# Two of the three passes of the experts' gate and up products made as one 512-column matmul

## The chip, the cores and the metric

The kernel runs on one core of one Trainium2 chip. The metric is the device time of an execution in microseconds; several runs of the same program are taken and their median is compared. Every product of the kernel is float32 in quality: operands are split into a high and a low part, and float32r passes of TensorE (PE in the profile) are summed in PSUM.

## The reference, cut to what matters

The program is one layer of an encoder: mixers (a long convolution, neighbourhood attention, pooling), an output projection, and then a mixture of 16 experts where each expert chooses 256 of the 2048 tokens. Only the experts matter here:

```
aff = softmax(h @ w_router)
gate, idx = top_k(aff.T, 256)          # per expert
xs = h[idx]                            # 16 x 256 x 1024
a = xs @ w_gate                        # 1024 -> 2048, per expert
b = xs @ w_up                          # 1024 -> 2048, per expert
y = (silu(a) * b) @ w_down * gate      # 2048 -> 1024, per expert
out = scatter-add of y at idx
```

## The kernel before, in words

The kernel works through stages: input projections, filter and convolution, attention, output projection and router, the search for each expert's tokens, and the experts (method `experts`, from L1055). This text deals with the last of them.

**Weights.** Each expert's weights (24 MB) come from HBM in 24 pieces of 1 MB. Helper `weights` (L1073) issues the transfer on SP's queue into `mo_raw`, and `split` (L208) makes two parts: ScalarE (ACT) copies to float32r `mo_wh` (L210), VectorE (DVE) subtracts to get `mo_wl` (L211). `mo_raw`, `mo_wh` and `mo_wl` have three buffers each, so the parts of a piece can be made once PE is done with the piece three before it.

**Gate and up.** For each eighth `f` of the 2048 hidden columns there are two pieces, first of w_gate, then of w_up. This text calls the work of one piece a tile. A tile has two halves `m` of 128 hidden columns, 8 chunks `d` of the 1024 inputs, and three passes each, by `mm3` (L213 to L217): 48 matmuls with the weights stationary and 256 tokens moving. `mm3` is

```
mm(out, lhsT=lh, rhs=rh, ...)   # L215: high weights, high tokens
mm(out, lhsT=lh, rhs=rl, ...)   # L216: high weights, low tokens
mm(out, lhsT=ll, rhs=rh, ...)   # L217: low weights, high tokens
```

The sums of a tile, 128 x 2 x 256, fill one PSUM bank. The tag `mm` has 6 banks, `tp` has 2 for transposes (L1332). After both tiles of an `f`, ACT applies Silu from PSUM to `mo_s` (L1149), DVE multiplies by the other bank (L1150), and `split` writes the parts `mo_hh` and `mo_hl` for the down product.

**Down.** Eight pieces of w_down, each with 24 matmuls of 512 columns by the same `mm3`, sum into four banks. ACT scales them into `mo_y` (L1172), and POOL adds the rows to the accumulator in DRAM (L1173).

**Lookahead.** At f = 3 the program emits the next expert's tokens: DVE makes 16 one-hot arrays (L1085), PE turns them into indices by 32 tiny matmuls (L1089), DVE finishes the indices (L1095), POOL issues two gathers of 128 rows, `mo_xg` (L1101). When they land, PE transposes them, four 128 x 128 blocks to a bank, two banks for each gather (L1117), and `split` writes `mo_xh` and `mo_xl`. DVE also copies the gate column from each gather (`mo_gt`, L1121).

What sets the order on each engine is a planner that simulates the program as it is emitted. Each engine then executes its own list in that order. Thus an instruction that waits also holds all behind it on its engine.

Of the kernel before, what the change touches and what calls it, by code (L numbers as in the profile page):

```python
# [33 lines left out]
def _parts(m):  # L34
    """Two parts of a float32 array of at most 12 significant bits each."""
    m = np.ascontiguousarray(m).astype(np.float32)
    h = ((m.view(np.uint32) + np.uint32(0x800)) & np.uint32(0xFFFFF000)).view(np.float32)
    return h, m - h


def _consts():
    """Arrays that depend on the shapes alone."""
# [31 lines left out]
    # rows (s, cs, n2), columns (cs', s, k2)  # L74
    z = np.zeros((4, 2, 16, 2, 4, 16))
    # rows (cs', s, k2), columns (s, cs, n2)
# [14 lines left out]
    # slot 0: frequency 0 and 2048; slots 1..7: 256 k2; slots 8..15: 128 + 256 (k2 - 8)  # L91
# [48 lines left out]
    # the candidates of a search by base-4 digits: four phases of 4, 4, 4 and 3 digits, each phase  # L140
    # in units of 2**-9 of the phase before
    # and half a unit less than the last of them
# [11 lines left out]
def _layouts(a):  # L154
    """Small inputs side by side, each in its own type, and the position biases in reverse."""
    f = np.zeros((128, 451), np.float32)
    f[0:33, 0:64] = a["hy_f_w1"][0]
    for h in range(2):
        r = slice(h * 64, h * 64 + 64)
        f[r, 64 + h * 64:128 + h * 64] = a["hy_f_w2"][0]  # L160
        f[r, 192:448] = a["hy_f_wout"][0][:, h * 256:h * 256 + 256]
        for q, n in enumerate(("hy_f_b1", "hy_f_b2", "hy_f_freq")):
            f[r, 448 + q] = a[n][0]
    g = np.zeros((128, 258), np.float32)
    for k in range(4):
        r = (k % 2) * 64
        g[r:r + 64, (k // 2) * 128 + r:(k // 2) * 128 + r + 64] = a["pool_w"][0][k]
    g[:, 256:258] = a["pool_scale"][0].reshape(2, 128).T
    h = np.zeros((128, 26), np.float32)
    h[:, 0:18] = a["hy_short_w"][0].reshape(3, 6, 128).transpose(2, 1, 0).reshape(128, 18)  # L170
    h[:, 18:24] = a["hy_short_b"][0].reshape(6, 128).T
    h[:, 24:26] = a["hy_skip"][0].reshape(2, 128).T
    rpb = a["na_rpb"][0][:, ::-1, ::-1].reshape(2, 4, 15, 31).transpose(0, 2, 1, 3)
    return {"par_f": f, "par_p": g, "par_h": h, "rpb_r": np.ascontiguousarray(rpb).reshape(120, 31)}


def _bc(ap, n, rows=128):
    """A DRAM vector of n elements, the same on every partition."""
    return bass.AP(tensor=ap.tensor, offset=ap.offset, ap=[[0, rows], [1, n]])


class Trunk:
# [16 lines left out]
    def rms(self, pool, ss, n, w):  # L199
        """rstd from sums of squares over n elements."""  # L200
        a = self.sb(pool, [128, w], f"rms_a{w}", bufs=2)
        self.nc.gpsimd.tensor_scalar(a, ss, 1.0 / n, EPS, op0=OP.mult, op1=OP.add)
        r = self.sb(pool, [128, w], f"rms_r{w}", bufs=2)
        self.nc.gpsimd.tensor_tensor(r, a, self.mhalf[:, 0:w], op=OP.pow)
        self.mark = self.nc.cur_bb.bb.instructions[-1]
        return r

    def split(self, hi, lo, src):  # L208
        """hi + lo = src exactly, each with at most 12 significant bits."""
# [9 lines left out]
    # ------------------------------------------------------------------ input projections  # L219
    def prep(self, pool, early, chunk, out):  # L220
        """x -> RMS norm, transposed and split, for 512 tokens."""
# [25 lines left out]
    def proj(self, pool, early):  # L247
        """x -> RMS norm -> w_in, 1024 tokens at a time; every product as three float32r passes."""
# [33 lines left out]
    def copy_values(self, half):  # L282
        """One copy of the values for each block of key columns."""
# [4 lines left out]
    def slab(self, pool, s, m, chunk, wh, wl, hh, hl):  # L288
        """Half a slab of columns of w_in for 512 tokens."""
# [18 lines left out]
        if s in (3, 4):  # L308
            # negated and scaled queries, in the order (column block, row, column)
# [24 lines left out]
    # ------------------------------------------------------------------ long filter and its spectrum  # L334
    def filt(self, pool):
# [13 lines left out]
        def sine(out, src, b):  # L349
            # the argument in turns, less its nearest whole number  # L350
# [61 lines left out]
    def to_groups(self, ev, dst, a, n0, pa):  # L412
        """Rows (k1, part) of two residues go to DRAM as [group][(k1 of 4, part, n2)][channel]."""
# [4 lines left out]
    # ------------------------------------------------------------------ hyena  # L418
    def hyena(self, pool):
# [49 lines left out]
        for g4 in range(8):  # L469
# [3 lines left out]
            # the real parts and the imaginary parts of the filter, each in both halves  # L473
# [8 lines left out]
            else:  # L482
                # frequencies 0 and 2048 share a slot and are real
# [57 lines left out]
    # ------------------------------------------------------------------ pooling  # L541
# [49 lines left out]
    # ------------------------------------------------------------------ neighbourhood attention  # L591
# [4 lines left out]
    def bias_tables(self, pool):  # L596
        """Negated position biases for each kind of column block and each first row of a window, rows
        and columns of keys in descending order: [first row][(query column, half of the heads)]
        [7 rows of BIG, the window, 7 rows of BIG][head][key column]."""
# [7 lines left out]
        # first query, number, offset of the window, offset among the biases: both step with the query  # L607
# [25 lines left out]
    def load_bias(self, tb, hg, rb, cb):  # L633
        """The biases of one block of queries for four heads, [key row][head][key column], over the 15 key
        rows around the block; only the query rows for which they differ from the block before."""
# [3 lines left out]
        # first query row, number, first window row and its step, first row of the source and its step,  # L639
        # first row of the tile, number of rows  # L640
# [8 lines left out]
    def attention(self, kpool, get_pool):  # L649
# [6 lines left out]
        # the low parts of the queries meet the high parts of the keys only  # L656
# [14 lines left out]
        def load(u):  # L671
            """Keys, queries and biases for four heads, eight rows and two blocks of columns."""
# [4 lines left out]
            if g == 0:  # L677
                k = kb([128, 4, 960], "at_k", R, 2)
                have = 0
                if rb:  # L680
                    # rows that the window shares with the one before it
# [43 lines left out]
        for u, (hg, rb, g) in enumerate(units):  # L725
# [16 lines left out]
            for j, cb in enumerate(self.QB[g * 2:g * 2 + 2]):  # L742
# [5 lines left out]
                for h in range(4):  # L748
# [26 lines left out]
                    else:  # L775
                        # two heads at a time, each in its half of the array's columns
# [5 lines left out]
                    if h == 3:  # L782
                        nc.scalar.activation(o[:, :, :, c0:c0 + 16], po.rearrange("p a (r c) -> p a r c", r=8), AF.Copy)
                        if g and j:
# [4 lines left out]
                            # what each query's exponentials sum up to goes into the norm's input  # L789
# [13 lines left out]
    # ------------------------------------------------------------------ output projection, router  # L803
    def load_wo(self, pool):
        """w_out, its rows scaled by the gains of the mixers' norms."""
# [23 lines left out]
    def mix(self, pool, chunk, bufs=1):  # L829
        """The outputs of the mixers for 256 tokens, split, and the rstd of each mixer."""  # L830
# [32 lines left out]
    def out_proj(self, pool, ready):  # L863
# [3 lines left out]
        # the router's weights, their rows scaled by the gains of the norm, both parts side by side  # L867
# [12 lines left out]
        def route(chunk, tiles, xh, xl, rs):  # L880
            """Affinities of one or two tiles of tokens."""
# [13 lines left out]
            else:  # L895
                # the last tile the shorter way
# [60 lines left out]
    # ------------------------------------------------------------------ the 256 tokens of each expert  # L957
    def top_tokens(self, pool):
        """Exact: the 256th largest affinity by a search over its bits, equal ones by token order."""
# [11 lines left out]
        def digits(ph):  # L971
            # a part of the 30 bits as a whole number of at most 8 bits, in the units of its phase
# [13 lines left out]
        for ph, n in enumerate(DIGITS):  # L986
            if ph == 0:
                v = part[0]
            else:
                # above the threshold so far: more than any candidate; below it: less than zero  # L990
# [5 lines left out]
            for k in range(n):  # L996
                # two candidates are counted, of the third the numbers below it less those above it
# [28 lines left out]
        # slots: first those above the threshold, then those on it, each in token order from 1;  # L1026
        # what lies on it beyond the capacity gets a slot above the capacity
# [26 lines left out]
    # ------------------------------------------------------------------ experts  # L1054
    def experts(self, pool):  # L1055
# [50 lines left out]
        def lookahead(e):  # L1106
            """The tokens of expert e, transposed and split."""
            idx, xg = tokens(e)
            gate = sb([128, 2], "mo_gt", F, 2)
            xh = sb([128, 8, 256], "mo_xh", R, 2)  # L1110
            xl = sb([128, 8, 256], "mo_xl", R, 2)
# [10 lines left out]
            return idx, gate, xh, xl  # L1122
# [6 lines left out]
        for e in range(NE):  # L1129
            idx, gate, xh, xl = nxt  # L1130
            hh = sb([128, 16, 256], "mo_hh", R, 1)
            hl = sb([128, 16, 256], "mo_hl", R, 1)
            for f in range(8):
# [6 lines left out]
                for src in (wg, wu):  # L1140
                    w, wlo = weights(src[e, :, :, f * 256:f * 256 + 256])
                    pt = self.bank("mm", (128, 2, 256))
                    for m in range(2):
                        ms = slice(m * 128, m * 128 + 128)
                        for d in range(8):
                            self.mm3(pt[:, m, :], w[:, d, ms], wlo[:, d, ms], xh[:, d, :], xl[:, d, :], d == 0, d == 7)
                    acc.append(pt)
                s = sb([128, 2, 256], "mo_s", F, 2)
                nc.scalar.activation(s, acc[0], AF.Silu)  # L1149
# [4 lines left out]
            po = [[self.bank("mm") for n in range(2)] for h in range(2)]  # L1154
# [44 lines left out]
    # ------------------------------------------------------------------ all of it  # L1199
    def run(self, stages=("all",), dbg=None):  # L1200
        tc, nc = self.tc, self.nc
        from contextlib import ExitStack
        with ExitStack() as st:
# [36 lines left out]
            def steps(gen, n=None):  # L1240
                """Advance a generator by n steps or to its end."""
# [90 lines left out]
            psa = psum("psum_d", mm=6, tp=2)  # L1332
# [32 lines left out]
```

## Time and profile before

| what | us |
|---|---|
| median of 3 runs | 3441.17 |
| lowest and highest run | 3441.08, 3451.25 |
| span of the profiled execution | 3444.6 |

The profiled execution has no separate time beside its span: from its first to its last instruction it took 3444.6 us, 3.4 us more than the median and inside the range of the runs. PE is busy 95% of it, DVE 51%, ACT 40%. Since matmuls overlap in the records and their ends are modelled, what counts for PE is the step from one start to the next.

### The profile page before, as it was taken

What the parts mean: (1) busy time and instruction counts of PE and PEld (TensorE: products, weight loads), DVE (VectorE), ACT (ScalarE), POOL (GpSimd) and SP (SyncE); (2) the same over time, 40 slices, a digit from 0 to 9 for tenths busy, and PEclk for the clock granted to TensorE, in tenths of its full rate; (3) what the DMA queues carried; (4) which work ended last, traced back from release to release, by engine and by line L of the source; (5) the groups of instructions that cost most, each with busy time, mean ns of one, the idle gap of its engine ahead of it and who ended that gap; (6) DMA issues with size and microseconds to landing.
All of it is one profiled execution on the core that took longest, in us unless ns stands there. A gap on an engine that the chain in (4) does not pass through costs nothing.

```text
span 3444.6 us, 52588 instructions
## 1 busy us (share of the span) xinstructions
PE 3267.8 (95%) x21970; PEld 2940.5 (85%) x21970; DVE 1747.9 (51%) x2296; ACT 1379.7 (40%) x1748; POOL 386.2 (11%) x466
## 2 busy tenths in 40 slices
PE   8999999687999599999999999999999999999998
PEld 6888887465688499899999999999989999899997
DVE  5124456254576654454544545545455454454455
ACT  4134422254432344444444444443434444444354
POOL 1212212121211000010010000100001001000011
PEclk9999999797999699999999999999999999999999
DMA  6675697887454356566566665665656656566586
GB/s 218 215 253 191 214 306 251 182 183 167 146 170 140 127 195 201 191 197 200 192 196 197 195 197 192 199 200 181 203 188 197 203 189 205 184 199 199 181 288 238
DMA packets 455158, 685.99 MB, mean 199 GB/s; under 512 B 27447, under 2 KB 366117, under 8 KB 454537
## 3 DMA queue, kind: packets, MB, share of 16 engines
q1 hardware_dynamic: 397592, 537.77, 50.4%
q0 software_dynamic: 28432, 103.26, 10.2%
q10 hardware_dynamic: 28896, 41.61, 3.5%
q8 instruction: 172, 2.82, 0.3%
q14 instruction: 66, 0.53, 0.0%
HBM read 578.05 MB, written 114.83 MB: 201 GB/s over the span
## 4 chain that ended last, share of the span: by engine, by line
PE 69%; issue 16%; DMA 12%; DVE 2%; ACT 0%; SPq 0%; POOL 0%; POOLq 0%; DVEq 0%; ACTq 0%
PE mm L215 20%; PE mm L217 20%; PE mm L216 20%; DMA mo_xg<-Hr,mo_ix 4%; DMA at_t<-Ce 4%; PE o L779 1%; DMA t<-Hd 1%; PE tp L765 1%; PE tp L1117 1%; PE s L752 0%; DMA at_v<-Vc 0%; DMA at_q<-QHd 0%; PE tp L395 0%; PE fl L529 0%; DVE tk_ge L1001 0%
## 5 line engine op out<-in xcount | busy, mean ns | idle before, releaser
L211 DVE TENSOR_TENSOR mo_wl<-mo_raw,mo_wh 128x2048 fp32r<-128x2048 f32 x384 | 879.9, 2292 | 798.4 <-ACT mo_wh L210 798.4
L210 ACT ACTIVATE mo_wh<-mo_raw 128x2048 fp32r<-128x2048 f32 x384 | 735.3, 1915 | 1210.8 <-issue 764.1
L215 PE MATMUL mm<-mo_xh,mo_wh 128*128 128x256 f32 x4096 | 1163.6, 284 | 0.0
L216 PE MATMUL mm<-mo_xl,mo_wh 128*128 128x256 f32 x4096 | 1162.5, 284 | 0.0
L217 PE MATMUL mm<-mo_xh,mo_wl 128*128 128x256 f32 x4096 | 1162.3, 284 | 0.0
L215 PEld LDWEIGHTS mm<-mo_xh,mo_wh 128*128 128x128 f32 x4096 | 788.3, 193 | 0.8 <-ACT mo_xh L210 0.2
L216 PEld LDWEIGHTS mm<-mo_xl,mo_wh 128*128 128x128 f32 x4096 | 788.4, 192 | 0.6
L217 PEld LDWEIGHTS mm<-mo_xh,mo_wl 128*128 128x128 f32 x4096 | 788.4, 192 | 0.0
L215 PE MATMUL mm<-mo_wh,mo_hh 128*128 128x512 f32 x1024 | 398.5, 389 | 0.0
L216 PE MATMUL mm<-mo_wl,mo_hh 128*128 128x512 f32 x1024 | 398.5, 389 | 0.0
L217 PE MATMUL mm<-mo_wh,mo_hl 128*128 128x512 f32 x1024 | 398.3, 389 | 0.0
L1173 POOL DMA_INDIRECT Acc<-mo_y,mo_ix x30 | 76.1, 2538 | 1412.8 <-ACT mo_y L1172 1292.6
L217 PEld LDWEIGHTS mm<-mo_wh,mo_hl 128*128 128x128 f32 x1024 | 192.2, 188 | 40.1
L215 PEld LDWEIGHTS mm<-mo_wh,mo_hh 128*128 128x128 f32 x1024 | 192.3, 188 | 39.6
L216 PEld LDWEIGHTS mm<-mo_wl,mo_hh 128*128 128x128 f32 x1024 | 192.3, 188 | 39.2
L215 PE MATMUL mm<-hT_h,w_h 128*128 128x512 f32 x512 | 205.7, 404 | 2.1 <-ACT hT_h L210 1.7
L216 PE MATMUL mm<-hT_l,w_h 128*128 128x512 f32 x512 | 205.3, 401 | 0.0
L217 PE MATMUL mm<-hT_h,w_l 128*128 128x512 f32 x512 | 204.3, 399 | 0.0
L1150 DVE TENSOR_TENSOR mo_s<-mo_s,mm 128x512 f32<-128x512 f32 x128 | 87.9, 687 | 183.5 <-PE mm L217 183.5
L1101 POOL DMA_INDIRECT mo_xg<-Hr,mo_ix x32 | 62.8, 1963 | 625.9 <-DVE mo_ix L1095 621.0
L215 PEld LDWEIGHTS mm<-hT_h,w_h 128*128 128x128 f32 x512 | 96.4, 189 | 26.0 <-ACT hT_h L210 2.4
L216 PEld LDWEIGHTS mm<-hT_l,w_h 128*128 128x128 f32 x512 | 96.3, 188 | 25.3 <-issue 2.8
(303 smaller groups left out, 3760.2 us busy)
## 6 DMA issues: line engine op xcount, KB each, us to landing
mo_raw<-in_w_gate SPq DMA_DIRECT2D x128, 1024.0 KB
mo_raw<-in_w_up SPq DMA_DIRECT2D x128, 1024.0 KB
mo_raw<-in_w_down SPq DMA_DIRECT2D x128, 1024.0 KB
w_r<-in_w_in SPq DMA_DIRECT2D x40, 512.0 KB
x<-in_x SPq DMA_DIRECT2D x16, 512.0 KB
Ud<-e ACTq DMA_DIRECT2D x32, 256.0 KB
at_q<-QHd SPq DMA_DIRECT2D x32, 256.0 KB
wo_x<-in_x SPq DMA_DIRECT2D x16, 512.0 KB
```

Source lines behind the costliest of these rows:

```text
L210: self.nc.scalar.activation(hi, src, AF.Copy)
L211: self.nc.vector.tensor_tensor(lo, src, hi.bitcast(F), op=OP.subtract)
L215: mm(out, lhsT=lh, rhs=rh, start=start, stop=False)
L216: mm(out, lhsT=lh, rhs=rl, start=False, stop=False)
L217: mm(out, lhsT=ll, rhs=rh, start=False, stop=stop)
L765: nc.tensor.transpose(pt[0:n * nkc, ci, :], s[:, x * nkc:(x + n) * nkc], self.ident)
L779: nc.tensor.matmul(po[hh % 2 * 64:hh % 2 * 64 + 64, h // 2, :], lhsT=v[0:n * nkc, ci, hh * 64:hh * 64 + 64], rhs=pp[0:n * nkc, ci, :], sta ...
L1101: nc.gpsimd.indirect_dma_start(out=g, out_offset=None, in_=self.Hr, in_offset=bass.IndirectOffsetOnAxis(ap=idx[:, h:h + 1].bitcast(U32), a ...
L1117: nc.tensor.transpose(pt[:, d, :], xg[h][:, dd * 128:(dd + 1) * 128], self.ident)
L1150: nc.vector.tensor_tensor(s, s, acc[1], op=OP.mult)
L1173: nc.gpsimd.indirect_dma_start(out=self.Acc, out_offset=off, in_=y, in_offset=None, compute_op=OP.add)
```

## The change: what it does

The high and low parts of the tokens are written side by side into one tile `mo_xx`. For each chunk, the high weights meet both parts in one matmul with 512 moving columns; its two halves go to the two halves of one PSUM bank. The low weights meet the high tokens as before, 256 columns, and add to the second half. So a tile has 32 matmuls instead of 48, with the same number of columns, and its sums take two banks. They are added when they are evicted: ACT copies the second half of both banks to `mo_s`, and DVE adds the first halves to it, once for gate and once for up. Silu and the multiplication then read SBUF. `mo_s` gets three buffers; the six banks become three pairs, and the down product takes two pairs. The rest of the diff removes comments.

```
-            xh = sb([128, 8, 256], "mo_xh", R, 2)
-            xl = sb([128, 8, 256], "mo_xl", R, 2)
+            xx = sb([128, 8, 2, 256], "mo_xx", R, 2)
+            xh, xl = xx[:, :, 0], xx[:, :, 1]
...
-                    pt = self.bank("mm", (128, 2, 256))
+                    pt = self.bank("mm", (128, 2, 2, 256))
                     for m in range(2):
                         ms = slice(m * 128, m * 128 + 128)
                         for d in range(8):
-                            self.mm3(pt[:, m, :], w[:, d, ms], wlo[:, d, ms], xh[:, d, :], xl[:, d, :], d == 0, d == 7)
-                    acc.append(pt)
-                s = sb([128, 2, 256], "mo_s", F, 2)
-                nc.scalar.activation(s, acc[0], AF.Silu)
+                            nc.tensor.matmul(pt[:, m].rearrange("p k t -> p (k t)"), lhsT=w[:, d, ms],
+                                             rhs=xx[:, d].rearrange("p k t -> p (k t)"), start=d == 0, stop=False)
+                            nc.tensor.matmul(pt[:, m, 1], lhsT=wlo[:, d, ms], rhs=xx[:, d, 0], start=False, stop=d == 7)
+                    a = sb([128, 2, 256], "mo_s", F, 3)
+                    nc.scalar.activation(a, pt[:, :, 1], AF.Copy)
+                    nc.vector.tensor_tensor(a, a, pt[:, :, 0], op=OP.add)
+                    acc.append(a)
+                s = acc[0]
+                nc.scalar.activation(s, s, AF.Silu)
                 nc.vector.tensor_tensor(s, s, acc[1], op=OP.mult)
...
-            po = [[self.bank("mm") for n in range(2)] for h in range(2)]
+            pair = [self.bank("mm", (128, 2, 512)) for h in range(2)]
+            po = [[pair[h][:, n] for n in range(2)] for h in range(2)]
...
-            psa = psum("psum_d", mm=6, tp=2)
+            psa = psum("psum_d", mm=3, tp=2)
```

## Rows read from the trace of the kernel before

**Rows 1.** Page: span, and part 2 (the span in 40 slices).
```profile
span 3444.6 us, 52588 instructions
...
PE   8999999687999599999999999999999999999998
```

**Rows 2.** Experts: stretch, length; busy us of PE, PEld, DVE, ACT, POOL; clock, DMA, GB/s.
```profile
1180.00:3420.00 2240.00, 2212.22 (x16047) 2089.93 (x16048) 1150.15 (x1035) 947.61 (x794) 155.34 (x94) 1.00 0.64 201
```

**Rows 3.** Waits of PE in that stretch: us in total, times, longest.
```profile
PE tp L1117 <- DVE mo_xl L211: 23.9, 14, 2.9
PE tp L1117 <- DMA mo_xg<-Hr,mo_ix: 13.0, 2, 9.4
```

**Rows 4.** Timeline of PE inside a gate tile: start us, duration, instruction.
```profile
2060.06 0.28 PE L216 MATMUL mm<-mo_xl,mo_wh 128*128 128x256 f32 x1
...
2060.18 0.28 PE L217 MATMUL mm<-mo_xh,mo_wl 128*128 128x256 f32 x1
...
2060.30 0.28 PE L215 MATMUL mm<-mo_xh,mo_wh 128*128 128x256 f32 x1
```

**Rows 5.** Timeline of ACT: making of weights, gate and up tiles, then down pieces.
```profile
2055.03 1.92 ACT L210 ACTIVATE mo_wh<-mo_raw 128x2048 fp32r<-128x2048 f32 x1 [3.33 <-issue]
...
2060.79 1.92 ACT L210 ACTIVATE mo_wh<-mo_raw 128x2048 fp32r<-128x2048 f32 x1 [3.36 <-issue]
...
2004.55 1.92 ACT L210 ACTIVATE mo_wh<-mo_raw 128x2048 fp32r<-128x2048 f32 x1 [3.52 <-PE mm L217]
...
2020.87 1.92 ACT L210 ACTIVATE mo_wh<-mo_raw 128x2048 fp32r<-128x2048 f32 x1 [3.52 <-PE mm L217]
```

**Rows 6.** Timeline of POOL: the first scatter of successive experts.
```profile
2164.72 1.92 POOL L1173 DMA_INDIRECT Acc<-mo_y,mo_ix  x1 [85.60 <-ACT mo_y L1172]
...
2304.64 2.04 POOL L1173 DMA_INDIRECT Acc<-mo_y,mo_ix  x1 [85.47 <-ACT mo_y L1172]
...
2447.50 2.04 POOL L1173 DMA_INDIRECT Acc<-mo_y,mo_ix  x1 [88.29 <-ACT mo_y L1172]
```

**Rows 7.** Page, part 5: matmuls of gate and up, and the product of the halves.
```profile
L215 PE MATMUL mm<-mo_xh,mo_wh 128*128 128x256 f32 x4096 | 1163.6, 284 | 0.0
...
L1150 DVE TENSOR_TENSOR mo_s<-mo_s,mm 128x512 f32<-128x512 f32 x128 | 87.9, 687 | 183.5 <-PE mm L217 183.5
```

**Rows 8.** ACT groups of one expert, 2026.3 to 2166.3: count, busy us, mean ns, idle before.
```profile
L210 ACT ACTIVATE mo_hh<-mo_s 128x512 fp32r<-128x512 f32 x8 | 4.9, 615 | 1.8 <-DVE mo_s L1150 1.8
L1149 ACT ACTIVATE mo_s<-mm 128x512 f32<-128x512 f32 x8 | 4.6, 579 | 0.0
```

**Rows 9.** Timeline of DVE: one tile's low weights, then a lookahead.
```profile
2062.74 2.29 DVE L211 TENSOR_TENSOR mo_wl<-mo_raw,mo_wh 128x2048 fp32r<-128x2048 f32 x1 [1.12 <-ACT mo_wh L210]
...
2085.02 0.15 DVE L1121 COPY mo_gt<-mo_xg 128x1 f32<-128x1 f32 x1 [5.49 <-DMA mo_xg<-Hr,mo_ix]
...
2087.34 1.28 DVE L211 TENSOR_TENSOR mo_xl<-tp,mo_xh 128x512 fp32r<-128x512 f32 x2
2088.54 0.68 DVE L1150 TENSOR_TENSOR mo_s<-mo_s,mm 128x512 f32<-128x512 f32 x1
```

**Rows 10.** Timeline of PE in that lookahead: index matmuls, transposes.
```profile
2072.18 0.95 PE L1089 MATMUL tp<-mo_tok,mo_oh 128*128 128x2 bf16 x32
...
2079.91 1.03 PE L1117 MATMUL tp<-ident,mo_xg 128*128 128x128 f32 x8
...
2088.08 0.66 PE L1117 MATMUL tp<-ident,mo_xg 128*128 128x128 f32 x4 [1.51 <-DVE mo_xl L211]
```

**Rows 11.** Timeline of PE: transposes of two other lookaheads.
```profile
2369.50 0.66 PE L1117 MATMUL tp<-ident,mo_xg 128*128 128x128 f32 x4 [2.85 <-DVE mo_xl L211]
...
2512.40 0.66 PE L1117 MATMUL tp<-ident,mo_xg 128*128 128x128 f32 x4 [2.89 <-DVE mo_xl L211]
```

**Rows 12.** Stretches after those waits (columns of rows 2; the clock is third from the end).
```profile
2372.00:2375.00 3.00, 3.00 (x19) 3.00 (x18) 2.64 (x4) 0.28 (x1) 0.00 (x0) 0.63 0.85 229
...
2515.00:2518.00 3.00, 3.00 (x27) 3.00 (x26) 2.54 (x4) 0.18 (x1) 0.00 (x0) 1.00 0.84 236
```

More of the change, by code (lines that the diff above doesn't have):

```diff
@@ L1121, in lookahead @@
                 nc.vector.tensor_copy(gate[:, h:h + 1], xg[h][:, D + e:D + e + 1])
-            return idx, gate, xh, xl
+            return idx, gate, xx
         nxt = lookahead(0)
@@ L1129, in experts @@
         for e in range(NE):
-            idx, gate, xh, xl = nxt
+            idx, gate, xx = nxt
             hh = sb([128, 16, 256], "mo_hh", R, 1)
```

## The prediction, made before the result was known

> **What bounds the kernel now.** I read the page first: from the fifteenth of its 40 slices on PE is busy nine tenths or more to the end [rows 1]. The stretch view of the experts says the same in numbers: of 2240 us PE is busy 2212, DVE 1150, ACT 948; the clock is 1.00, the DMA engines work at 0.64 of their time [rows 2]. A busy PE is not yet a bound, so the waits come next. In that stretch PE waited for others in 16 places only, 36.9 us together, all before the transposes of a lookahead [rows 3]; no matmul of gate, up or down waited for weights or for a bank. The bound is therefore PE's own steps. A gate or up matmul starts 0.12 us after the one before, pass after pass [rows 4]. Finer: ACT makes the next weights whenever a tile ends, and these starts lie 5.76 us apart [rows 5], which over 48 matmuls is 120.0 ns each. Down pieces come every (2020.87 - 2004.55) / 3 = 5.44 us [rows 5], over 24 matmuls 226.7 ns each, with 512 columns. So 256 further columns cost 106.7 ns (2.4 GHz), and each matmul has 13.3 ns besides, whatever its columns. An expert takes 139.9 us [rows 6], of which 16 x 5.76 + 8 x 5.44 = 135.7 are such steps; the rest is index matmuls, transposes and the one wait.
>
> **The matmuls.** A triple of passes took 3 x 120.0 = 360.0 ns. It becomes one step of 512 columns and one of 256: 226.7 + 120.0 = 346.7 ns. The columns are the same; one fixed cost of 13.3 ns is gone. There are 4096 triples (16 experts, 16 tiles, 16 each) [rows 7], so 4096 x 13.3 = 54.6 us leave the path that sets the end. The bounds of this term: nothing, if the fixed cost stays in another form, and 54.6. I take all of it, since the 512-column step is measured in the same stage, with a new stationary operand before every matmul, as here.
>
> One page speaks against so much. The Trainium skill, "TensorE: Matmul & The Clock Gate", section "Wait — 56ns, not 53.3ns?", puts the fixed cost of a matmul at about 2.5 ns at the full clock; by it the removed matmuls would be worth an estimated 10 us. This case's trace disagrees, with 13.3 ns at both widths.
>
> **Eviction, ACT.** Added are 256 copies of 128x512 from PSUM; the nearest rows are Silu from PSUM, 0.58 us, and the copy into `mo_hh`, 0.62 [rows 8]. Silu itself stays, from SBUF. 256 x 0.6 = 154 us bring ACT from 948 to about 1100 of some 2190: half its time. **Eviction, DVE.** Added are 256 additions with one operand in PSUM, like the multiplication at 0.687 us [rows 7]: 176 us, 1150 to 1326, six tenths. Neither becomes the bound, and both lie beside PE's work. I cost them at nothing on the path. What hides them is the lead of the weights: ACT starts on the parts for a tile three ahead when a tile ends (2060.79) and DVE is done with them at 2062.74 + 2.29 = 2065.03 [rows 5, 9], while PE needs them two tiles later, at 2072.31; the lead is 7.3 us, with tiles of 5.55 us it is 6.9. In an ordinary `f` ACT and DVE gain at most 1.3 and 1.4 us of work per two tiles, well inside it. If that cover went, 1.4 us would cost 128 times as much, 179 us.
>
> **Banks.** Three pairs instead of six banks: a tile may begin when the tile three before it is evicted, two tile times (11.1 us) after that one's end. The eviction takes a copy and an addition, 0.6 + 0.7 us, behind at most one making of weights on each engine (1.9 and 2.3 us): 5.5 us. Nothing on the path. The down product takes pairs that were freed two tiles earlier. Its eviction may wait for both halves of a pair if the pair is treated as one; after the last expert that is one step of 0.7 us at most, which I leave in the range.
>
> **Transfers.** The same bytes in less time: 5.55 us for 1 MB in gate and up; down already runs at 5.44 us for 1 MB without a wait of PE. Nothing on the path.
>
> **The lookahead.** This is the one place where the cover is thin. PE makes the indices at 2072.18, and the second gather lands at 2085.02, where DVE has stood still for 5.49 us at the gate column; then DVE makes low weights (2.29 us), frees the first `tp` bank, and PE, which came to the second gather's transposes 1.51 us before, goes on at 2088.08 [rows 9, 10]. The gather's time does not shrink with PE's steps. Between the index matmuls and these transposes PE has about 103 matmuls ((2088.08 - 1.51 - 2072.18 - 0.95 - 1.03) / 0.12), 34 triples, which become 34 x 13.3 = 0.46 us shorter; so PE waits 0.46 us longer in each of 15 lookaheads, 6.9 us. Besides, an addition that is due may stand ahead of the bank's release on DVE: between nothing and two of them, 0 to 1.38 us each time, 0 to 21 us. In the rows the next eviction on DVE (2088.54) stands behind the release [rows 9], so I take nothing for it and keep the 21 for the range. The planner may as well place the transposes later, and up to 27.5 us of the present waits (36.9 without the 9.4 ahead of the first expert) would go.
>
> **Sum.** -54.6 + 6.9 = -47.7 us. Against the profiled execution, 3444.6 - 47.7 = 3396.9; it stands 3.4 us over the median of the runs, so the forecast for a median is 3441.2 - 47.7 = 3393.5 us.
>
> **Rivals.** (1) The lookahead's wait grows until the clock falls. Two waits of 2.85 and 2.89 us are in the trace [rows 11]; after the first the clock was 0.63 in the next full stretch, after the second it stayed at 1.00 [rows 12]. The expert with the fall took 142.9 us against 139.9 [rows 6], 1.35 of it by the longer wait, some 1.6 by PE at 1.2 GHz. If all 15 lookaheads went that way: 15 x 2.95 = 44 us given back, 3441.2 - 54.6 + 44 = 3431. For it: a wait of 1.51 + 0.46 + one addition of 0.69 is 2.66, near those two. Against: even at that length one of two kept its clock. Chance 0.08.
>
> (2) The wait goes, because the planner puts the transposes elsewhere: 3441.2 - 54.6 - 27.5 = 3359. For it: the list of PE is made anew. Against: 15 lookaheads show the same pattern, since the landing is later than the plan takes it to be. Chance 0.07.
>
> (3) The fixed cost is not saved: a 512-column matmul whose two halves belong to different sums, or a narrow one behind it, takes 13 ns more than the rows say; with no saving left 3441 to 3448 with the longer waits, with a fifth left 3431 to 3437. Against: the 512-column step of down and all three passes of gate show one fixed cost. By the page's 2.5 ns, this is the case that would come; the rows give it little. Chance 0.04.
>
> (4) Slower: weights come late behind ACT. Silu now waits for a DVE addition, not for PE. If that addition stands on DVE behind the gate column that waits for the gather (5.49 us) and behind low weights (2.29), ACT stands at Silu up to 8.5 us, and the next making of high weights behind it; over the lead of 6.9 us PE then waits for weights. It decides from 54.6 / 15 = 3.6 us for each expert; at 6 us it would give 3441.2 - 54.6 + 90 = 3477. For it: the 5.49 us stand in every lookahead. Against: a single hold of 8.5 would exceed the lead by 1.6 us only, and two would have to meet. Chance 0.04.
>
> **Numbers.** The forecast has the remaining 0.77: 3386.6 (no longer wait) to 3415 (0.46 and two additions in each lookahead), 3393.5 the likeliest. The range takes half of rival 2 below, 3373, and a few falls of the clock above, 3418. About 0.3% (10 us) is what a measurement of this kernel can tell from no change. Faster by more than that: forecast, (1) for the most part and (2), 0.91; within: (3) and the rest of (1), 0.05; slower: 0.04.
>
> **What would show it.** Right: tiles of gate and up 5.55 us apart on ACT, a matmul of 512 columns every 347 ns, experts near 137 us, PE waiting only before transposes and about 2 us there, DVE busy near 60%. Wrong: a step of the pair over 355 ns; PE waiting for `mo_wl` or for an addition that frees a bank; waits before transposes of 3 us with the clock at 1.2 GHz behind them.

## The result and the profile after

The changed kernel is faster by 1.8%: median 3382.06 us against 3442.59 us of the kernel before (four runs each), ratio 0.9818, 95% interval 0.9804 to 0.9832. That is 60.5 us less; 47.7 were forecast, and the range (3373 to 3418) holds it. The profiled execution took 3379.5 us against 3444.6 before. The way there is only partly the one that was forecast.

The page of the changed kernel: span, part 1, and two groups of part 5.

```profile
span 3379.5 us, 44817 instructions
...
PE 3228.9 (96%) x17874; PEld 2715.2 (80%) x17874; DVE 1903.2 (56%) x2552; ACT 1522.2 (45%) x2004; POOL 354.2 (10%) x466
...
L1153 DVE TENSOR_TENSOR mo_s<-mo_s,mm 128x512 f32<-128x512 f32 x256 | 174.0, 680 | 0.0
L1152 ACT ACTIVATE mo_s<-mm 128x512 f32<-128x512 f32 x256 | 147.9, 578 | 0.0
```

PE has 4096 matmuls fewer (17874 against 21970). The evictions cost what was worked out: 174 us on DVE (176 forecast), 148 on ACT (154). The stretch of the experts (columns as in [rows 2]):

```profile
1180.00:3360.00 2180.00, 2175.41 (x11969) 1866.66 (x11970) 1304.46 (x1290) 1089.08 (x1049) 123.08 (x94) 1.00 0.65 206
```

DVE works 60% of it and ACT 50%, as forecast; PE is still the bound. Its waits in that stretch, which answer to [rows 3]:

```profile
PE tp L1117 <- DMA mo_xg<-Hr,mo_ix: 2.7, 1, 2.7
PE tp L1117 <- DVE mo_xx L211: 1.4, 1, 1.4
PE mm L1148 <- DVE mo_xx L211: 0.6, 1, 0.6
PE mm L1148 <- DVE mo_s L1153: 0.3, 1, 0.3
```

Without the wait of 9.4 us before the first expert (in this trace it lies just outside the stretch), 27.5 us of waits became 5.0, where 6.9 us more were forecast. The timeline of PE shows the wide matmuls of a tile; each pair is a wide step and a narrow one:

```profile
2035.73 0.40 PE L1148 MATMUL mm<-mo_xx,mo_wh 128*128 128x512 f32 x1
...
2036.79 0.40 PE L1148 MATMUL mm<-mo_xx,mo_wh 128*128 128x512 f32 x1
...
1199.80 0.39 PE L1148 MATMUL mm<-mo_xx,mo_wh 128*128 128x512 f32 x1
...
1200.84 0.40 PE L1148 MATMUL mm<-mo_xx,mo_wh 128*128 128x512 f32 x1
```

From each first row to its second are three pairs: 1.06 us, 353 ns each, in the one place, and 1.04 us, 347 ns, in the other. By the starts of all pairs, about seven tenths take 353 and three tenths 347, on average 351.3. So the merged matmul brings 4096 x (360 - 351.3) = 35.6 us, not 54.6. An expert, by POOL's first scatters (to be compared with [rows 6], 139.9 us), takes 136.49 and 135.71 us:

```profile
2000.14 1.62 POOL L1181 DMA_INDIRECT Acc<-mo_y,mo_ix  x1 [84.63 <-ACT mo_y L1180]
...
2136.63 1.62 POOL L1181 DMA_INDIRECT Acc<-mo_y,mo_ix  x1 [85.28 <-ACT mo_y L1180]
...
2272.34 1.62 POOL L1181 DMA_INDIRECT Acc<-mo_y,mo_ix  x1 [84.63 <-ACT mo_y L1180]
```

### The profile page after: what moved, and what is told of

It is laid out like the page before. It is cut to its first block, busy times and chain, and to the rows that moved or that the text cites. A ratio compares the mean times of both kernels' runs of the same rounds, so it can differ in the third digit from the quotient of the medians.

```text
span 3379.5 us, 44817 instructions
## 1 busy us (share of the span) xinstructions
PE 3228.9 (96%) x17874; PEld 2715.2 (80%) x17874; DVE 1903.2 (56%) x2552; ACT 1522.2 (45%) x2004; POOL 354.2 (10%) x466
## 4 chain that ended last, share of the span: by engine, by line
PE 87%; DMA 9%; DVE 2%; issue 1%; ACT 1%; SPq 0%; POOL 0%; POOLq 0%; DVEq 0%; ACTq 0%
PE mm L1148 28%; PE mm L1150 14%; PE mm L215 12%; PE mm L216 12%; PE mm L217 12%; DMA at_t<-Ce 3%; DMA t<-Hd 1%; PE o L779 1%; PE tp L765 1%; DMA at_q<-QHd 1%; PE tp L1117 1%; PE s L752 1%; DMA at_v<-Vc 1%; DMA mo_xg<-Hr,mo_ix 1%; DMA at_q<-QLd 0%
## 5 line engine op out<-in xcount | busy, mean ns | idle before, releaser
L1148 PE MATMUL mm<-mo_xx,mo_wh 128*128 128x512 f32 x4096 | 1445.1, 397 | 0.8 <-DVE mo_xx L211 0.6
L1150 PE MATMUL mm<-mo_xx,mo_wl 128*128 128x256 f32 x4096 | 1151.1, 281 | 0.0
L1148 PEld LDWEIGHTS mm<-mo_xx,mo_wh 128*128 128x128 f32 x4096 | 770.0, 188 | 185.4 <-DVE mo_xx L211 1.0
L1150 PEld LDWEIGHTS mm<-mo_xx,mo_wl 128*128 128x128 f32 x4096 | 774.5, 189 | 0.7
L1181 POOL DMA_INDIRECT Acc<-mo_y,mo_ix x30 | 68.5, 2283 | 1395.9 <-ACT mo_y L1180 1278.7
L1156 ACT ACTIVATE mo_s<-mo_s 128x512 f32<-128x512 f32 x128 | 81.0, 633 | 235.8 <-DVE mo_s L1153 235.8
L1153 DVE TENSOR_TENSOR mo_s<-mo_s,mm 128x512 f32<-128x512 f32 x256 | 174.0, 680 | 0.0
L1152 ACT ACTIVATE mo_s<-mm 128x512 f32<-128x512 f32 x256 | 147.9, 578 | 0.0
L216 PEld LDWEIGHTS mm<-hT_l,w_h 128*128 128x128 f32 x512 | 96.2, 188 | 25.3 <-issue 2.8
L217 PEld LDWEIGHTS mm<-hT_h,w_l 128*128 128x128 f32 x512 | 96.2, 188 | 23.8 <-issue 1.8
```

What stands on the lines that cost most here:

```text
L216: mm(out, lhsT=lh, rhs=rl, start=False, stop=False)
L217: mm(out, lhsT=ll, rhs=rh, start=False, stop=stop)
L1148: nc.tensor.matmul(pt[:, m].rearrange("p k t -> p (k t)"), lhsT=w[:, d, ms], rhs=xx[:, d].rearrange("p k t -> p (k t)"), start=d == 0, sto ...
L1150: nc.tensor.matmul(pt[:, m, 1], lhsT=wlo[:, d, ms], rhs=xx[:, d, 0], start=False, stop=d == 7)
L1152: nc.scalar.activation(a, pt[:, :, 1], AF.Copy)
L1153: nc.vector.tensor_tensor(a, a, pt[:, :, 0], op=OP.add)
```

## The experiments

Theory A: the gain has two sources, some 35 us from the merged matmul and the rest from waits that the new plan happens not to have. Rivals: all of it is the matmul; all of it is the plan. Two kernels take the sources apart.

**The matmul cut in two again** (all else as changed):

```
-  nc.tensor.matmul(pt[:, m].rearrange(...), lhsT=w[:, d, ms], rhs=xx[:, d].rearrange(...), ...)
+  for k in range(2):
+      nc.tensor.matmul(pt[:, m, k], lhsT=w[:, d, ms], rhs=xx[:, d, k], start=d == 0 and k == 0, stop=False)
```

> The changed kernel with its 512-column matmul cut into two of 256 columns; pairs of banks, eviction and buffers stay changed. Theory A (the gain of 60 us has two sources: about 34 us from the merged matmul, 4096 times 360 less about 351.6 ns, and about 22 us from the waits before the transposes, which the new plan no longer has): triples of 360 ns again, waits still near 5 us, 3416 us, 3405 to 3425. Rival B (all of it is the merged matmul, 13.3 ns or more each): 3437 to 3443. Rival C (all of it is the plan and its waits): 3380 to 3386.

Measured: 3422.86 us, ratio to the kernel before 0.9941 (0.9924 to 0.9958), inside the range of theory A and outside those of both rivals.

**The kernel before, with its transposes later:**

```
-                    nxt = lookahead(e + 1)
+                    ahead = tokens(e + 1)
+                if f == 4 and e + 1 < NE:
+                    nxt = lookahead(e + 1, ahead)
```

> The kernel before, with the transposes and splits of the next expert's tokens emitted at f = 4 instead of f = 3 (the indices and gathers stay at f = 3). Theory A: the waits before the transposes, 27.5 us, go or nearly go, triples stay at 360 ns, 3417 to 3425. Rival B: no change, 3438 to 3445, the waits only move to another place.

Measured: 3410.18 us, ratio 0.9910 (0.9890 to 0.9930), some 7 us below what theory A expected. The start of the experts is PE's first group of index matmuls; these are the rows of the kernel before, of the changed one, of the cut one and of the one with later transposes, in this order.

```profile
1167.34 3.55 PE L1089 MATMUL tp<-mo_tok,mo_oh 128*128 128x2 bf16 x32 [0.84 <-DVE mo_oh L1085]
```
```profile
1164.64 3.55 PE L1089 MATMUL tp<-mo_tok,mo_oh 128*128 128x2 bf16 x32 [0.84 <-DVE mo_oh L1085]
```
```profile
1170.35 3.55 PE L1089 MATMUL tp<-mo_tok,mo_oh 128*128 128x2 bf16 x32 [0.84 <-DVE mo_oh L1085]
```
```profile
1163.06 3.55 PE L1089 MATMUL tp<-mo_tok,mo_oh 128*128 128x2 bf16 x32 [0.84 <-DVE mo_oh L1085]
```

From there to the end of the spans (3444.6, 3379.5, 3419.8, 3406.3) the experts take 2277.3, 2214.9, 2249.5 and 2243.2 us. Putting the merged matmul in, with everything else of the change there, takes 34.6 us away; moving the transposes alone takes 34.0 away from the kernel before. Of the second, 26.4 us are waits that went. Besides, the trace of the kernel before has two stretches at 1.2 GHz behind its longest waits, 3.4 us [rows 12] and 6.8 us long, which cost half their length, 5.1 us; the one with later transposes has none. The last 2.5 us were not found. Both sources are real and of about the same size. Together they make 68.6 us and not 62.4, for the most part because the changed kernel kept one such wait before its last expert, 2.7 us, with 3.4 us at 1.2 GHz behind it. The stretches behind the waits before the last expert, in the kernel before and in the changed one (clock third from the end):

```profile
3208.00:3211.00 3.00, 3.00 (x15) 3.00 (x15) 2.01 (x2) 1.20 (x2) 0.00 (x0) 0.50 0.06 25
```
```profile
3146.00:3149.00 3.00, 2.84 (x12) 2.65 (x13) 1.60 (x4) 2.07 (x2) 0.00 (x0) 0.54 0.18 72
```

**The eviction done twice:**

```
                     acc.append(a)
+                    twice = sb([128, 2, 256], "mo_2", F, 2)
+                    nc.scalar.activation(twice, pt[:, :, 1], AF.Copy)
+                    nc.vector.tensor_tensor(twice, twice, pt[:, :, 0], op=OP.add)
```

> The changed kernel with the copy and the addition of each eviction done twice, the second time into a buffer that nothing reads: 256 more copies on ACT (148 us) and 256 more additions on DVE (174 us). Theory A (they lie beside PE's work): PE waits below 15 us, 3382 to 3392. Rival D (the eviction's cover is thin, each further addition is late for someone): over 3400, with waits of PE for banks or weights.

Measured: 3413.84 us, ratio 0.9916 (0.9900 to 0.9933), so rival D holds for this amount. PE's waits in the experts:

```profile
PE tp L1117 <- DMA mo_xg<-Hr,mo_ix: 11.6, 7, 2.5
PE mm L1148 <- DVE mo L1157: 7.0, 2, 6.6
PE mm L1148 <- DVE mo_gt L1121: 2.5, 1, 2.5
```

322 us of further work cost 28 us against the changed kernel (3385.73 in its own repeat below): no wait is for weights. In the traces, where the experts take 27 us longer, about 9 of them are waits for banks, 9 more waits before transposes, and 5 two falls of the clock, 6.8 us each, both around a wait for a bank; the rest was not found. The 6.6 us are a bank that comes free late: in the last expert DVE stood 5.74 us at the final normalisation, and the second addition (L1157) stood behind it.

```profile
3271.51 1.28 DVE L1199 SCALAR_TENSOR_TENSOR mo_y<-mo_xa,rms_r,mo_gf 128x1024 f32<-128x1024 f32 x1 [5.74 <-POOL rms_r L204]
...
3277.84 0.68 DVE L1157 TENSOR_TENSOR mo<-mo,mm 128x512 f32<-128x512 f32 x1
```

**Two pairs of banks instead of three** (`psum("psum_d", mm=2, tp=2)`):

> The changed kernel with two pairs of banks instead of three. A tile may now begin only when the tile two before it is evicted, one tile time (5.6 us) after its end, and the down product takes both pairs while the last two tiles are being evicted. By the prediction's step on banks the eviction ends at most 5.5 us after the tile: in gate and up PE waits little, up to 1 us for each expert where a gather holds DVE; at the start of down and at the start of the next expert one eviction each is not covered, 2 to 4 us for each expert. 30 to 80 us more than the changed kernel, 3412 to 3462. If three pairs were more than is needed: 3380 to 3390.

Measured: 3413.89 us, ratio 0.9917 (0.9900 to 0.9933). The time is in the expected range, but not for the reason given: the start of down and the next expert show no wait. PE waited 25.3 us before transposes (9.4 to 9.5 of it before the first expert, as always), and once 5.8 us for a bank in the last expert:

```profile
PE tp L1117 <- DMA mo_xg<-Hr,mo_ix: 25.3, 14, 9.5
PE mm L1148 <- DVE mo_s L1153: 5.8, 1, 5.8
```

Against the trace of the changed kernel the experts take 25 us longer: 13 are further waits before transposes, 5.5 the bank, some 2 a longer fall of the clock around it (6.8 us), and 5 were not found. So with three pairs PE hardly waits for a bank, and with two it does so once; half of what the smaller number costs comes from where this plan puts the transposes.

**Why 353 and not 347.** Three edits looked for it. First, the two halves of a tile in turn (`for d` outside, `for m` inside), so that successive pairs add into different banks:

> The changed kernel with the two halves of a tile in turn for each chunk d, so that successive pairs add into different banks. If 353 ns instead of 347 comes from a 512-column and a 256-column matmul adding one behind the other into the same bank: 347 ns, 15 to 20 us less, near 3365. If it is a state of PE that the banks don't set: no change, 3378 to 3388.

Measured: 3386.09 us, ratio 0.9827 (0.9809 to 0.9844), no change; an expert takes 136.49 us as before. So the bank of the pair before is not the cause. A wide matmul and its own narrow one still share a bank here; g1, below, has them apart.

```profile
2006.81 1.62 POOL L1181 DMA_INDIRECT Acc<-mo_y,mo_ix  x1 [84.63 <-ACT mo_y L1180]
...
2143.30 1.62 POOL L1181 DMA_INDIRECT Acc<-mo_y,mo_ix  x1 [85.28 <-ACT mo_y L1180]
```

Second, a tiny matmul ahead of each tile:

```
+  nc.tensor.matmul(pt[:, 0, 0, 0:2], lhsT=iota[:, 0:128], rhs=tok[:, 0, :], start=True, stop=True)
```

> The changed kernel with one tiny matmul (bf16, 2 columns, some 25 ns, its result overwritten) ahead of each of the 256 tiles of gate and up. If the two step lengths of a pair, 347 and 353 ns, are a state that tiny matmuls and transposes switch, as the places in the trace suggest: the share of the two changes, tiles of 5.55 and 5.65 us in another mixture, between 14 us less and 14 us more than the changed kernel with 6 us for the tiny matmuls themselves. If the state depends on what the tile reads or writes: the mixture stays as it is and the time grows by 6 us, near 3388.

Measured: 3420.86 us, ratio 0.9941 (0.9918 to 0.9964); both expectations missed. Tiles became 5.78 us (the next two rows), 0.13 more than 16 pairs of 353 ns, so a tiny matmul costs five times the 25 ns that it takes from start to start in a row of 32 such [rows 10], mostly because the wide step right behind it takes 313 ns; and the pairs came back to 353 within a few steps nearly everywhere. A state that a tiny matmul moves for good is ruled out.

```profile
2021.23 0.18 PE L1145 MATMUL mm<-mo_tok,mo_iota 128*128 128x2 bf16 x1
...
2027.01 0.18 PE L1145 MATMUL mm<-mo_tok,mo_iota 128*128 128x2 bf16 x1
```

Third, eight of a kind in a row:

```
                             nc.tensor.matmul(pt[:, m]..., rhs=xx[:, d]..., start=d == 0, stop=False)
+                        for d in range(8):
                             nc.tensor.matmul(pt[:, m, 1], lhsT=wlo[:, d, ms], rhs=xx[:, d, 0], start=False, stop=d == 7)
```

> The changed kernel with the eight 512-column matmuls of a half first and its eight 256-column ones after them, instead of in turn. If a step depends on its own width alone, and the 353 ns that most pairs take come from a state that PE falls into whatever the order: 512-column steps of 227 or 233 ns, 256-column steps of 117 to 120, and 3382 us within 5. If the alternation of widths costs the 5 ns over 346.7: pairs at 346.7 ns, 4096 x 5 = 20 us less, 3362.

Measured: 3422.04 us, ratio 0.9935 (0.9917 to 0.9953); both expected times were missed. It is slower than the changed kernel by waits that this order's plan has before the transposes of every lookahead and by falls of the clock behind 11 of the 15. PE's waits, and the stretch behind one of them, which was 2.1 us long (clock third from the end):

```profile
PE tp L1117 <- DMA mo_xg<-Hr,mo_ix: 31.6, 15, 2.2
```
```profile
1381.00:1384.00 3.00, 2.98 (x15) 2.98 (x16) 1.85 (x4) 0.91 (x2) 0.00 (x0) 0.53 0.15 57
```

Its steps answer a part of the question. The timeline of PE, single starts of the first wide matmuls of a half, its last, and the first two narrow ones behind it:

```profile
1901.34 0.40 PE L1148 MATMUL mm<-mo_xx,mo_wh 128*128 128x512 f32 x1
1901.57 0.40 PE L1148 MATMUL mm<-mo_xx,mo_wh 128*128 128x512 f32 x1
1901.81 0.39 PE L1148 MATMUL mm<-mo_xx,mo_wh 128*128 128x512 f32 x1
...
1902.95 0.39 PE L1148 MATMUL mm<-mo_xx,mo_wh 128*128 128x512 f32 x1
1903.18 0.28 PE L1151 MATMUL mm<-mo_xx,mo_wl 128*128 128x256 f32 x1
```

The eight wide steps read one by one are 233, 236, 229, 232, 231, 227, 226 and 227 ns, then the narrow ones 113, 119 and six of 120; the medians over all halves are the same within 1 ns. So 227 and 120 are reached, but the wide ones get there only some five steps after a change of width; widths in turn (230 to 241 and 112 to 120 in the changed kernel) never settle. A pair takes 349 ns here: both answers offered were half right.

**Late transposes in the changed kernel** (the edit shown above):

> The changed kernel with the transposes and splits of the next expert's tokens emitted at f = 4 (as was tried on the kernel before). If both sources of the gain are separate and the changed kernel has already lost nearly all of its waits: the remaining 5 us of waits and one fall of the clock go, pairs stay at 347 to 353 ns, 2 to 8 us less than the changed kernel, 3374 to 3382. If the moved transposes are worth 30 us here too (as in the kernel before): near 3352.

Measured: 3386.17 us, ratio 0.9835 (0.9818 to 0.9851): no gain, 4 us above what was expected. The waits after the first 9.5 us went to 2.8 us, but more of the pairs took 353 ns, nearly nine tenths, 352.4 on average (an expert 136.54 and 136.29 us). The 30 us of the kernel before are not there a second time.

**Both together.** If widths in a row save steps and late transposes remove the waits, the two belong together; g1 has sixteen of a kind in a row (a whole tile), g2 eight, and g3 is the changed kernel again.

> The changed kernel with all sixteen 512-column matmuls of a tile first, then its sixteen of 256 columns, and with the transposes of the next expert's tokens emitted at f = 4. From the steps with eight of a kind in a row, where a 512-column step falls from 234 to 227 ns and a 256-column step rises from 113 to 120 after each change of width: 16 x 226.7 + 27 + 16 x 120.0 - 7 = 5567 ns for a tile, 348 ns for a pair instead of 352, 16 us less than the changed kernel, and no waits before transposes: 3364 to 3372. If the plan brings waits back, or the widths in turn cost nothing: 3382 or more.

> The same with eight of a kind in a row (one half of a tile at a time): 8 x 226.7 + 27 + 8 x 120.0 - 7 = 2794 ns for a half, 349.2 ns for a pair, 11 us less than the changed kernel if the late transposes take away the waits that this order had (31.6 us with falls of the clock): 3369 to 3378. If those waits belong to the order of the matmuls itself: near 3415.

> The changed kernel itself, beside the other two on the same chip: 3379 to 3388, ratio to before 0.982.

Measured, on one chip: g2 3369.93 us, ratio 0.9797 (0.9780 to 0.9815); g3 3385.73, ratio 0.9835 (0.9821 to 0.9848); g1 3445.32, ratio 1.0000 (0.9989 to 1.0011). A half of g2 takes 2.79 us as worked out (timeline of PE, eight of a kind merged into a row):

```profile
2029.18 2.00 PE L1147 MATMUL mm<-mo_xx,mo_wh 128*128 128x512 f32 x8
...
2031.97 2.00 PE L1147 MATMUL mm<-mo_xx,mo_wh 128*128 128x512 f32 x8
```

g1 lost everything to the mechanism of rival (1). PE's waits, the transposes of one lookahead in its timeline, and the stretches before and behind them (clock third from the end):

```profile
PE tp L1116 <- DMA mo_xg<-Hr,mo_ix: 46.3, 13, 3.7
```
```profile
1665.88 1.42 PE L1116 MATMUL tp<-ident,mo_xg 128*128 128x128 f32 x8 [3.54 <-DMA mo_xg<-Hr,mo_ix]
```
```profile
1663.00:1666.00 3.00, 0.12 (x1) 0.12 (x2) 0.14 (x1) 0.15 (x1) 0.00 (x0) 1.00 1.06 397
1666.00:1669.00 3.00, 3.00 (x13) 2.61 (x14) 1.84 (x3) 1.20 (x2) 0.00 (x0) 0.58 0.13 49
```

The steps of g1 also take the bank and the width apart. Its sixteen wide matmuls go from one half and its bank to the other after eight, and steps 9 to 16 stay at 227 ns; its first narrow one adds into another bank than the wide one before it, and the narrow steps are 113, 119 and 120 ns as with eight in a row, where it is the same bank. The first steps are long or short after a change of width, not of bank.

**g1 with the transposes at f = 5** tests that this was all that ailed it:

> The kernel with sixteen of a kind in a row, its transposes emitted at f = 5 instead of f = 4. Its tiles took 5.57 us as worked out, and its time was lost in waits of 3.7 us before the transposes and the falls of the clock behind them. If those are the whole of it: no waits, 3362 to 3370, some 75 us less than with f = 4 and about 5 less than the version with eight in a row. If something else in that order costs the time (evictions, weights): over 3400.

Measured: 3368.01 us, ratio 0.9772 (0.9759 to 0.9785), faster than the kernel before and the changed one, and 77 us less than with f = 4. The traces account for it: g1 has 48 us more of waits, and 13 falls of the clock, 58 us at 1.2 GHz together, which cost 29 us. Beyond the first expert's 9.4 us PE waits 2.2 us:

```profile
PE tp L1116 <- DMA mo_xg<-Hr,mo_ix: 9.4, 1, 9.4
PE tp L1116 <- DVE mo_xx L211: 1.6, 1, 1.6
PE mm L1147 <- DVE mo_xx L211: 0.6, 1, 0.6
```

## Why the prediction was right, and where it was not

**What bounds the kernel: right.** PE's steps set the time in every version; in the experts no wait for weights shows in any trace.

**The matmuls: right in kind, too large.** The term "4096 x 13.3 = 54.6 us" came from a 512-column step of 226.7 ns, read where all steps are wide. In turn with narrow ones the pair takes 347 or 353 ns instead of 346.7, and the term measured 34.6 us by the cut kernel. The trace of before had a warning that the prediction did not use: in a stretch of the input projections with wide steps only, three take 0.70 us, 233 ns each:

```profile
249.79 0.39 PE L215 MATMUL mm<-hT_h,w_h 128*128 128x512 f32 x1
...
250.49 0.40 PE L215 MATMUL mm<-hT_h,w_h 128*128 128x512 f32 x1
```

The cut kernel also bears on the fixed cost of 2.5 ns in the Trainium skill ("TensorE: Matmul & The Clock Gate", section "Wait — 56ns, not 53.3ns?"), with which this term would be an estimated 10 us: the measured one is over three times that.

**Eviction: right as long as there is room.** The sums for ACT and DVE agree within 4%, and no wait of PE for a bank above 0.3 us shows. Doubling them shows that the room is finite, and that it ends at the lookahead and the last expert, not at the weights, where the prediction had put the cover.

**The lookahead: the step that failed.** "The gather's time does not shrink with PE's steps", so PE would wait 6.9 us longer; in fact 22.5 us of waits went, as in rival (2), which had a chance of 0.07. The step took the place of the transposes and the pace of the gather from the old plan as fixed, and the new plan changed both. It also read the old pattern as more even than it is: of the 15 lookaheads 13 wait as described, the first not at all, and the last one 3.5 us for the gather itself, with 6.8 us at 1.2 GHz behind it, a fall that rival (1) does not count. Two things changed in the new plan. PE reaches the second gather's transposes 16.2 us after the index matmuls (14.4 before):

```profile
2046.33 0.95 PE L1089 MATMUL tp<-mo_tok,mo_oh 128*128 128x2 bf16 x32
...
2062.57 1.03 PE L1117 MATMUL tp<-ident,mo_xg 128*128 128x128 f32 x8
```

And the gather was quicker. Timeline of the kernel before, then of the changed one: POOL's second gather, the making of low weights on DVE, SP's next weights.

```profile
2076.00 2.28 DVE L211 TENSOR_TENSOR mo_wl<-mo_raw,mo_wh 128x2048 fp32r<-128x2048 f32 x1
2076.10 3.02 POOL L1101 DMA_INDIRECT mo_xg<-Hr,mo_ix  x1 [0.30 <-issue]
...
2078.31 0.37 SPq L1075 DMA_DIRECT2D mo_raw<-in_w_up  x1
```
```profile
2050.26 1.09 POOL L1101 DMA_INDIRECT mo_xg<-Hr,mo_ix  x1 [0.30 <-issue]
2050.75 2.28 DVE L211 TENSOR_TENSOR mo_wl<-mo_raw,mo_wh 128x2048 fp32r<-128x2048 f32 x1
...
2053.05 0.37 SPq L1075 DMA_DIRECT2D mo_raw<-in_w_up  x1
...
2055.81 0.15 DVE L1121 COPY mo_gt<-mo_xg 128x1 f32<-128x1 f32 x1 [1.46 <-DMA mo_xg<-Hr,mo_ix]
```

Before, POOL began the gather inside the low weights, finished 0.84 us after them, behind a new transfer of 1 MB, and the gather landed 8.9 us after its start; changed, it began ahead of both and landed after 5.5. Both patterns hold in 13 lookaheads of their kernel; in two of those before, the gather took 10.2 us to land, and these have the waits of 2.85 and 2.89 us. That the later place alone suffices is shown by the experiment on the kernel before: there these gathers still take 3.02 us and land some 8.9 us after their start. What the quicker gather alone is worth was not tried.

**The sum** came out by luck, because the two errors have opposite signs: 54.6 - 34.6 = 20 too much, 6.9 + 22.5 = 29 too little, and 3 more for the clock (10.2 us at 1.2 GHz in the experts before, 3.4 after), which leads from 3393.5 to about 3381, against 3382 measured. **Rivals:** (1) did not come here but for the last lookahead; g1 is it in full; (2) came; (3) came for a third of the term (20 of 54.6 us); (4) did not come.

## What to carry to other kernels

Take a matmul's fixed cost from steps in the same mixture of widths, and keep matmuls of one width in a row where order is free. When a planner orders the work, any edit moves the places where an in-order engine meets a gather; price those places apart from the edit, and try the edit with them moved, since waits of 2 to 4 us that end in a fall of the clock can hide most of the gain or all of it (3422 and 3445 against 3368 to 3370 us here). Emitting a consumer of a gather one step later is a cheap change of its own: 35 us in the kernel before, nothing in the changed one.

## What was not expected of the hardware

The step of a matmul depends on the widths of those before it: 512 columns take 228 to 236 ns behind 256-column ones and 227 some five steps later, 256 columns 113 rising to 120. That is not all of it: in the stretch of the input projections shown above 512-column steps stay near 233 ns with none but wide ones before them, and in the down product they take 227. Why pairs in turn take 347 in some stretches and 353 in others stays open; the bank of the pair before is ruled out, and a tiny matmul does not choose.

A gather that POOL begins while DVE subtracts two SBUF operands into the low weights is held until that ends: 3.02 us instead of 1.09, ending 0.84 us after the subtraction. In all traces together 111 gathers begin so, and each ends 0.81 to 0.98 us after the subtraction, however early that began. The Trainium skill, "SBUF — State Buffer", section "Who interferes with whom", has a DVE instruction with two SBUF inputs contend with a GpSimd instruction that reads SBUF; these rows agree, for the gather reads its row numbers (`mo_ix`) from there.

The clock (2.4 GHz, or 1.2 when it falls) fell after PE waits of 3.54 us in g1 and 2.85 us in [rows 11], but not after one of 2.89 us; with eight of a kind in a row it fell after 11 of 15 waits of 1.9 to 2.2 us. The length of the wait alone does not decide it.
